# A decoder step on one core: operations listed first, issued at the end, with a table of moves on three engines

## The chip, the cores and the metric

One core of a Trainium2 chip runs the program. The time is the device time in microseconds (us) of one execution, the median of several. The engines are TensorE (PE in the profile, its weight loads PEld), VectorE (DVE), ScalarE (ACT), GpSimd (POOL) and SyncE (SP), whose queue issues all transfers. Each engine works through its own list of instructions in order; semaphores tie the lists together.

## The reference

One layer of a hybrid decoder, in float32, for 1024 tokens of a prompt and 8 single tokens of running sequences:

```python
p = x @ w_in                              # 1024 -> 9360 columns
p_gla, p_rwkv, p_gate = split(p)
o_gla  = gated linear attention of p_gla  # 4 heads, state 128 x 256, chunks
o_rwkv = RWKV-7 recurrence of p_rwkv      # 16 heads, state 64 x 64, token shift, group norm
m   = sigmoid(gate_a) * (o_gla @ w_up_gla) + sigmoid(gate_b) * (o_rwkv @ w_up_rwkv)
out = layernorm(alpha * x + m @ w_out)
```

The new states and the last shifted row are outputs too.

## The kernel before, in words

The prompt is worked in two passes of 512 tokens; the first also carries the 8 samples. Activations stand transposed: 128 columns of the projection on the partitions, tokens along the row. A float32 product is made of three products in a faster format: each operand is split into a high part (a cast on ACT: `xh`, `wpart`) and a low part (a subtraction on DVE: `xl`, `wpart`), and `hi*xh + hi*xl + lo*xh` is summed in a PSUM bank. `blocks` walks a plan of such 128-column blocks: first all of `w_in` for pass 0 and 1, then the two up-projections, then the output projection. A block takes a bank `proj` (2 of them) or `big` (5); `evacuate` copies the result out on ACT or DVE and frees the bank.

Beside this stream of large matmuls run, as Python generators, the small ones. `pair` handles two RWKV heads: `front` makes decays, keys (`kb`), the products `BK` (in tiles named `wide`) and `AZ` (`az`), and two sums over heads by a matmul with `headsr`, whose operand is split into two tiles `part`; the second of them sums `te`, a scalar_tensor_tensor of `r`, `rk` and `kb`. Four `big` banks of products are then masked into `gg`. `back` and `turn` invert small triangular blocks (`Xd`, `XT`, `Yd`) and turn the values; `chain` steps through 8 chunks with three matmuls each in the one bank `pch`; `norm` normalises and writes out. `gla_head` does the same for one attention head, `load_x` loads and splits the rows of the next stage's input.

What sets the order is the class `Order`. Every generator yields operations; each operation has an estimated cost and an estimated earliest start on its engine. `run` keeps asking all streams for their next operation, gives each a key (its start less a priority of its kind) and takes the smallest. So each engine's list is the order in which `run` took the operations. In the kernel before, `run` calls `op.fn()` at that moment, which issues the instruction. `take` hands out a buffer of a tag (the one idle longest by the estimates), `free` gives it back; the generators wait for buffers with `get`. All operations are issued through the same line of a helper, so nearly all instructions show one source line in the profile, and are told apart by their tiles.

Of the kernel before, what the change touches and what calls it, by code (L numbers as in the profile page):

```python
# [20 lines left out]
P = 128  # L21
# [73 lines left out]
STAND, SCARCE, PER_ROW = 0.033, 0.043, 0.107  # L95

URGENT = 1.952

STRETCH = 5
TUNED = {  # L100
# [29 lines left out]
SIGMOID, EXP = "sigmoid_and_others", "natural_log_exp_and_others"  # L130
# [45 lines left out]
class Op:  # L176


    def __init__(self, ways, out, ins, lag=0.0, table=None, tiles=None, port=""):
        self.ways, self.out, self.ins, self.lag, self.table, self.tiles = ways, out, ins, lag, table, tiles  # L180
        self.port, self.outs = port, [out]
        self.eng, self.fn, self.cost = ways[0]
# [123 lines left out]
class Order:  # L306
# [4 lines left out]
    def __init__(self, nc):  # L311
        self.P, self.A, self.V, self.G, self.S, self.E, self.C = (Engine(**e) for e in (
            {"P": nc.tensor}, {"A": nc.scalar}, {"V": nc.vector}, {"G": nc.gpsimd}, {"S": nc.sync},
            {"V": nc.vector, "G": nc.gpsimd}, {"A": nc.scalar, "V": nc.vector}))
        self.tiles = (P, P)
        self.quads = {"V": {}, "A": {}}
        self.time = dict.fromkeys("PAVGS", 0.0)
        self.port = dict.fromkeys("VG", 0.0)
        self.dma = 0.0
        self.flight = [0.0] * FLIGHT  # L320
        self.table = EXP
        self.ready, self.read = {}, {}
        self.streams, self.stretch = [], None
        self.tune(0)
        self.idle, self.make, self.home, self.wait = {}, {}, {}, {}
        self.kept, self.tile = {}, {}

    def tune(self, n):
# [4 lines left out]
            self.for_pe = {k: max(0.0, FOR_PE.get(k, 0.0) + x.get("pe " + k, 0.0)) for k in PRIO}  # L333

    def buffers(self, tag, bufs, make):
        self.idle[tag], self.make[tag], self.wait[tag] = [0.0] * bufs, make, 0

    def fixed(self, tag, tiles):

# [19 lines left out]
    def take(self, tag):  # L359
        idle = self.idle[tag]  # L360
        t = min(idle)
        idle.remove(t)
        x = self.make[tag]()
        self.home[x.tensor.name] = tag
        if tag in self.kept:
            self.tile[x.tensor.name] = x
        self.ready[x.tensor.name] = (t, None)
        return x

    def free(self, *xs):  # L370
        for x in xs:
            n = x.tensor.name
            tag = self.home.pop(n)
            self.idle[tag].append(max(self.ready.pop(n)[0], self.read.pop(n, 0.0)))
            if tag in self.kept:
                self.kept[tag].append(self.tile.pop(n))

# [21 lines left out]
    def start(self, op):  # L399

        best = None
        for eng, fn, cost in op.ways:
            free, t = self.time[eng] + (SWITCH if eng == "P" and op.tiles != self.tiles else 0.0), 0.0
            for x in (*op.outs, *op.ins):
                at, by = self.ready.get(x.tensor.name, (0.0, None))
                if eng == "S" and by == "D" and x is op.out:
                    continue
                if by != eng:
                    at += HOP.get(by, 0.0) + (SPARE if eng == "P" and by in ("V", "A", "G") else LANDED if by == "D" else 0.0)
                elif eng != "P" and x is not op.out:  # L410
                    at += AFTER[eng]
                t = max(t, at)
            t = max(t, *(self.read.get(x.tensor.name, 0.0) for x in (*op.outs, *(y for y in op.ins if y.space == PSUM))))
            if eng in op.port:
                free = max(free, self.port["G" if eng == "V" else "V"])
            if eng == "S":
                t = max(t, self.flight[-FLIGHT])
            late, t = free - t, max(t, free)
            if eng in "VA" and self.held(eng, op):
                cost += HOLD  # L420
            end = t + cost
            if len(op.ways) > 1:
                end += BIAS if eng == "V" and "A" in op.ways[0][0] else ASIDE if eng == "G" and "G" in op.port else 0.0
            if best is None or end < best[0]:
                best = end, t
                op.eng, op.fn, op.cost, op.late = eng, fn, cost, max(0.0, late)
        return best[1]
# [10 lines left out]
    def run(self):  # L438
        while self.streams:
            best, before = None, list(self.streams)  # L440
            self.urgent = self.needed()
            stand = max(STAND, SCARCE - PER_ROW * len(self.idle["row"]))
            for s in before:
                self.advance(s)
                if s.op is not None:
                    t = self.start(s.op)
                    if s.op.eng == "P":
                        key = t - stand * self.for_pe[s.kind] - (SWITCH if s.op.tiles != self.tiles else 0.0)
                    else:
                        key = t - self.prio[s.kind]  # L450
                    if s.kind in self.urgent:
                        key -= URGENT
                    if s.op.table not in (None, self.table):
                        key += max(0.0, TABLE - AGE * s.op.late)
                    if best is None or key < best[0]:
                        best = key, t, s
            if best is None:
                assert self.streams != before, "streams wait for one another"
                continue
            _, t, s = best  # L460
            op, s.op = s.op, None
            cost = op.cost
            if op.table not in (None, self.table):
                cost += TABLE
                self.table = op.table
                self.nc.scalar.preload_act_table_set(self.table)  # L466
            op.fn()
            self.time[op.eng] = max(self.time[op.eng], t + cost)
            if op.eng in op.port:
                self.port[op.eng] = t + cost  # L470
            if op.eng == "P":
                self.tiles = op.tiles
            elif op.eng in "VA":
                for x, q in self.starts(op):
                    self.quads[op.eng][x is op.out, x.space] = q
            end = t + cost
            if op.eng == "S":
                self.dma = max(self.dma, end) + op.lag[0]
                end = self.dma + op.lag[1]
                self.flight.append(end - EARLY)  # L480
            for x in op.outs:
                n = x.tensor.name
                self.ready[n] = max(end, self.ready.get(n, (0.0,))[0]), "D" if op.eng == "S" else op.eng
            for x in op.ins:
                n = x.tensor.name
                self.read[n] = max(self.read.get(n, 0.0), end)


class Kern(Order):
# [331 lines left out]
    def first_blocks(self, xs):  # L821

        run = []
        for b in self.plan[:2]:
            evac = yield from b.act()
            for tt, (t0, n) in enumerate(b.c.tiles):
                ps = yield from self.get("big")
                run.append((b, tt, t0, n, ps, evac))
        w, idle = {}, (yield from self.bank("pch", [P, P]))
        half = len(run) // 2  # L830
        for k, part in [(0, run[:half]), (1, run[:half]), (0, run[half:]), (1, run[half:])] + [(k, run) for k in range(2, NK)]:
            yield lambda: len(xs) > k
            for b, tt, t0, n, ps, evac in part:
                f0 = t0 - LEAD if b.lead and tt else t0
                q = ps[:, :t0 + n - f0]
                if tt == 0 and k % 4 == 0:
                    yield lambda: self.ws
                    w[id(b)] = self.ws.pop(0)
                hi, lo = (w[id(b)][:, v, k % 4 * P:k % 4 * P + P] for v in range(2))
                xh, xl = xs[k]  # L840
                yield self.P.matmul(q, hi, xh[:, f0:t0 + n], start=(k == 0), stop=False)
                yield self.P.matmul(q, hi, xl[:, f0:t0 + n], start=False, stop=False)
                yield self.P.matmul(q, lo, xh[:, f0:t0 + n], start=False, stop=(k == NK - 1))
                fin = tt == len(b.c.tiles) - 1
                if fin and k % 4 == 3:
                    yield from self.used(w[id(b)])
                if k == NK - 1:
                    self.spawn(self.evacuate(evac(tt, t0, n, q), ps, b.post if fin else None), "evacuate")
            for _ in range(IDLE if part is not run and part[0] is run[0] else 0):
                yield self.P.matmul(idle, self.warm, self.warm, start=True, stop=True)  # L850
            if k == 2:
                self.free(idle)
# [1104 lines left out]
```

## Time and profile before

| | us |
|---|---|
| median of 3 runs | 1434.02 (1433.89 to 1434.51) |
| the profiled execution, time | 1435.45 |
| the profiled execution, span | 1433.6 |
| PE busy in the span | 1417.2 |
| DVE, ACT, POOL busy | 1053.5, 827.3, 419.4 |
| granted TensorE clock, mean | 0.999 |

The span is from the first to the last instruction. "Busy" of PE is the time covered by at least one recorded matmul; since matmuls overlap in the record, a wait of PE shows there only with the part that no earlier matmul covers. A wait is named by the engine, the tile that the waiting instruction writes, and what ended the wait.

### The profile page before, as it was taken

Reading aid. Unit: us, or ns where it says so; the run is one execution under the profiler, and the core shown is the slowest. Engines: PE = TensorE matmul, PEld = TensorE weight load, DVE = VectorE, ACT = ScalarE, POOL = GpSimd, SP = SyncE. Lnnn points to the kernel's source line nnn. Section 1 sums busy time; section 2 is a strip of 40 time slices with the busy share of each in tenths; the row PEclk is TensorE's granted clock in tenths of the full one; section 3 lists DMA queues with packets and bytes.
Section 4 is the critical chain, followed back from the end, with each engine's and each line's share of the span. In section 5 each row is a group of like instructions: output and inputs, shape, how many; then the busy total and the mean of one; then the engine's idle time right before and its main releaser. Section 6 shows DMA issues by size and latency. Waiting matters only on the chain.

```text
span 1433.6 us, 30379 instructions
## 1 busy us (share of the span) xinstructions
PE 1417.2 (99%) x10640; PEld 1251.5 (87%) x10640; DVE 1053.5 (73%) x2125; ACT 827.3 (58%) x2070; POOL 419.4 (29%) x1156
## 2 busy tenths in 40 slices
PE   9999999999999999999999999999999999999997
PEld 8999999999999998888888887888888898897786
DVE  7688485978586978477668879788795946676685
ACT  6556666665658576556475646564667646654210
POOL 1060506261525250533512463265314050000000
PEclk9999999999999999999999999999999999999999
DMA  9798979686988786886688777577568597798732
GB/s 327 245 317 261 312 234 329 210 283 219 280 274 292 260 266 220 252 242 176 185 238 261 202 217 208 156 216 217 163 205 245 162 262 250 246 305 288 256 125 83
DMA packets 284789, 340.12 MB, mean 237 GB/s; under 512 B 159027, under 2 KB 174524, under 8 KB 284636
## 3 DMA queue, kind: packets, MB, share of 16 engines
q1 hardware_dynamic: 284636, 338.18, 75.0%
q8 instruction: 85, 1.39, 0.4%
q14 instruction: 68, 0.56, 0.1%
HBM read 210.03 MB, written 127.00 MB: 235 GB/s over the span
## 4 chain that ended last, share of the span: by engine, by line
PE 86%; DVE 6%; ACT 3%; DMA 2%; issue 1%; SPq 1%; POOL 0%; DVEq 0%; ACTq 0%; POOLq 0%
PE proj L273 54%; PE big L273 25%; PE pch L273 6%; DVE row L273 2%; ACT row L273 2%; DVE wide L273 1%; DVE wpart L273 1%; SPq L273 1%; DMA wraw<-w_in 1%; DVE gg L273 0%; DMA row<-lora 0%; ACT wpart L273 0%; ACT L466 0%; DVE Xd L273 0%; DVE XT L273 0%
## 5 line engine op out<-in xcount | busy, mean ns | idle before, releaser
L273 PE MATMUL proj<-xh,wpart 128*128 128x256 f32 (+3 forms) x3696 | 903.1, 329 | 0.9 <-DVE row L273 0.8
L273 PEld LDWEIGHTS proj<-xh,wpart 128*128 128x128 f32 x3696 | 617.2, 189 | 52.6 <-issue 5.5
L273 PE MATMUL proj<-xl,wpart 128*128 128x256 f32 (+3 forms) x1848 | 606.5, 328 | 0.1
L273 PEld LDWEIGHTS proj<-xl,wpart 128*128 128x128 f32 x1848 | 348.7, 189 | 26.9 <-issue 2.8
L273 POOL TENSOR_TENSOR Xt<-X,wide 128x60 f32<-128x60 f32 (+24 forms) x496 | 173.2, 349 | 285.3 <-DMA wide<-LD 201.5
L273 DVE TENSOR_TENSOR wpart<-wraw,wpart 128x512 fp32r<-128x512 f32 x206 | 143.6, 706 | 60.7 <-ACT wpart L273 52.9
L273 POOL TENSOR_TENSOR X<-X,Xt 128x60 f32<-128x60 f32 (+24 forms) x496 | 175.0, 353 | 38.7
L273 DVE TENSOR_TENSOR row<-row 128x256 f32<-128x256 f32 (+10 forms) x334 | 173.6, 533 | 11.5 <-ACT row L273 5.6
L273 ACT CAST wpart<-wraw 128x512 fp32r<-128x512 f32 x210 | 128.6, 620 | 73.9 <-PE proj L273 30.1
L273 ACT ACTIVATE row<-row 128x512 f32<-128x512 f32 (+5 forms) x229 | 138.0, 611 | 6.7 <-DVE row L273 3.9
L273 PE MATMUL big<-xh,wpart 128*128 128x256 f32 (+3 forms) x576 | 133.5, 319 | 0.2 <-DVE wpart L273 0.2
L273 POOL TENSOR_TENSOR row<-row 128x512 f32<-128x512 f32 (+4 forms) x35 | 40.0, 1153 | 300.7 <-DVE row L273 178.8
L273 ACT COPY row<-big 128x128 f32<-128x128 f32 (+6 forms) x187 | 61.9, 347 | 70.1 <-PE big L273 63.0
L273 PEld LDWEIGHTS big<-xh,wpart 128*128 128x128 f32 x576 | 95.3, 188 | 6.9 <-DVE wpart L273 0.4
L273 DVE TENSOR_TENSOR wide<-pch,gg 64x65 f32<-64x65 f32 x224 | 49.9, 223 | 60.1 <-PE pch L273 57.6
L273 PE MATMUL big<-xl,wpart 128*128 128x256 f32 (+3 forms) x288 | 91.7, 318 | 0.9 <-DVE xl L273 0.9
L273 DVE SCALAR_TENSOR_TENSOR row<-proj,pv,row 128x255 f32<-128x255 f32 (+1 forms) x95 | 54.6, 575 | 49.2 <-ACT tail L273 37.1
L273 ACT COPY rh<-pch 128x130 f32<-128x130 f32 x119 | 31.8, 267 | 96.3 <-PE pch L273 95.6
L273 ACT COPY wide<-pch 64x65 f32<-64x65 f32 x243 | 50.4, 207 | 51.4 <-PE pch L273 48.1
L273 PE MATMUL big<-row 128*64 128x64 f32 (+5 forms) x680 | 69.0, 287 | 0.1
L466 ACT ACT_TABLE_LOAD x52 | 66.7, 1283 | 0.9
L273 ACT ACTIVATE row<-proj,omu 128x256 f32<-128x256 f32 (+1 forms) x95 | 51.7, 544 | 23.3 <-PE proj L273 22.6
(222 smaller groups left out, 2044.3 us busy)
## 6 DMA issues: line engine op xcount, KB each, us to landing
w<-wpart SPq DMA_DIRECT2D x146, 512.0 KB
wpart<-w SPq DMA_DIRECT2D x146, 512.0 KB
wraw<-w_in SPq DMA_DIRECT2D x146, 256.0 KB
wide<-LD SPq DMA_DIRECT2D x64, 128.0 KB
BT<-row SPq DMA_DIRECT2D x32, 256.0 KB
wide<-BT SPq DMA_DIRECT2D x64, 128.0 KB
wraw<-w_up_gla SPq DMA_DIRECT2D x32, 256.0 KB
row<-w_out SPq DMA_DIRECT2D x32, 256.0 KB
```

Of the source, the lines that this page charges most:

```text
L273: ways.append((eng, lambda call=call: call(out, *args, **kw), price(eng, name, out, args, ins)))
L466: self.nc.scalar.preload_act_table_set(self.table)
```

## The change

`run` no longer issues. It appends each operation to a list, `issued`, with its engine, the names of the tensors that it writes and reads, and its table of functions on ACT. When all are listed, `issue` makes one list per engine, notes for every operation which earlier ones it needs (writers of what it reads or writes, readers of what it overwrites, and the last users of the buffer that its tile follows in, kept in `gone` and `follows`), and then edits the lists of PE ("P"), ACT ("A") and DVE ("V") by a table: an entry (n, k) takes the operation at place n and puts it back at place n + k. Then the lists are issued, always the earliest-listed operation that is next on its engine and whose needs are met. The operations, their engines, costs and the estimates by which `run` lists them are the same as before.

The table has 70 entries for PE, 50 for ACT and 109 for DVE; most places are 1 to 5. Two lines of it, and the new code:

```diff
+MOVES = {"P": [
+    (6, -4), (7, -4), (8, -4), (10, 4), (10, 3), (15, -4), (16, -4), (16, -1), (65, 3), (69, -3), (70, -2),
...
+         "V": [
...
+    (296, 2), (301, -1), (362, -2), (363, 4), (365, -1), (373, 2), (381, -4), (380, -2), (381, -2), (383, 2),
...
     def take(self, tag):
         idle = self.idle[tag]
         t = min(idle)
+        before = self.gone[tag].pop(idle.index(t))
         idle.remove(t)
         x = self.make[tag]()
+        self.follows[x.tensor.name] = before
...
             if op.table not in (None, self.table):
                 cost += TABLE
                 self.table = op.table
-                self.nc.scalar.preload_act_table_set(self.table)
-            op.fn()
+            self.issued.append((op.eng, op.fn, {x.tensor.name for x in op.outs}, {x.tensor.name for x in op.ins}, op.table))
...
+        self.issue()
+
+    def issue(self):
+
+        todo = {e: [] for e in "PAVGS"}
+        wrote, read, touch, needs = {}, {}, {}, []
+        for n, (eng, _, outs, ins, _) in enumerate(self.issued):
+            todo[eng].append(n)
+            need = {wrote[x] for x in outs | ins if x in wrote}
+            for x in outs | ins:
+                if x in self.follows and x not in touch:
+                    need.update(touch.get(self.follows[x], ()))
+                touch.setdefault(x, []).append(n)
+            for x in outs:
+                need.update(read.pop(x, ()))
+                wrote[x] = n
+            for x in ins - outs:
+                read.setdefault(x, []).append(n)
+            needs.append(need)
+        for eng, moves in MOVES.items():
+            for n, places in moves:
+                todo[eng].insert(n + places, todo[eng].pop(n))
+        loaded, done, at = EXP, set(), dict.fromkeys(todo, 0)
+        while len(done) < len(self.issued):
+            n = min(todo[e][k] for e, k in at.items() if k < len(todo[e]) and needs[todo[e][k]] <= done)
+            eng, fn, _, _, table = self.issued[n]
+            if table not in (None, loaded):
+                loaded = table
+                self.nc.scalar.preload_act_table_set(table)
+            fn()
+            done.add(n)
+            at[eng] += 1
```

Three places show what the table does to the lists. Buffer numbers differ between the two programs, so only the names and the order are to be compared.

The first is DVE in `front` of a pair in pass 0 (near 265 us in the trace of before). `pc` is a copy of decays, the four `wide` rows are the products into `BK`, the SCALAR_TENSOR_TENSOR is `te`, `part` the low part of its split, `Xd` the transposes of another pair's `back`. Before:

```order
L273 COPY pc_4079<-row_3829 128x8
L273 TENSOR_TENSOR wide_3813<-row_3830,row_3829 64x8x64
L273 TENSOR_TENSOR wide_3813<-row_3472,row_3829 64x8x64
L273 TENSOR_TENSOR wide_3813<-row_3830,row_3829 64x8x64
L273 TENSOR_TENSOR wide_3813<-row_3472,row_3829 64x8x64
L273 SCALAR_TENSOR_TENSOR row_3831<-row_3349,pv_88,row_3472 128x512
L273 TENSOR_TENSOR wpart_4069<-wraw_3976,wpart_4069 128x512
L273 TENSOR_TENSOR wpart_4132<-wraw_4010,wpart_4132 128x512
L273 TENSOR_TENSOR part_4124<-row_3831,part_4123 128x512
L273 STREAM_TRANSPOSE Xd0_184<-XT0_178 32x4x32 x4
```

and after:

```order
L303 COPY pc_812<-row_771 128x8
L303 TENSOR_TENSOR wide_763<-row_772,row_771 64x8x64
L303 TENSOR_TENSOR wide_763<-row_711,row_771 64x8x64
L303 SCALAR_TENSOR_TENSOR row_773<-row_693,pv_88,row_711 128x512
L303 TENSOR_TENSOR wide_763<-row_772,row_771 64x8x64
L303 TENSOR_TENSOR wide_763<-row_711,row_771 64x8x64
L303 TENSOR_TENSOR wpart_816<-wraw_803,wpart_816 128x512
L303 STREAM_TRANSPOSE Xd0_184<-XT0_178 32x4x32
L303 TENSOR_TENSOR part_815<-row_773,part_814 128x512
L303 STREAM_TRANSPOSE Xd0_184<-XT0_178 32x4x32
L303 TENSOR_TENSOR wpart_810<-wraw_797,wpart_810 128x512
```

`te` moved ahead of two of the products, and the second subtraction behind the `part` that follows from `te` and two transposes of `back`.

The second is DVE one pair later (near 340 us), where the four `big` banks are masked into `gg`; the TENSOR_TENSOR on `row` is the last product of `norm` for the pair before. Before:

```order
L273 STREAM_TRANSPOSE Xd0_184<-XT1_179 32x4x32 x4
L273 TENSOR_TENSOR row_4974<-row_4974,row_3698 128x512
L273 TENSOR_TENSOR gg_4970<-big_5283,cons_76 128x8x64
L273 TENSOR_TENSOR gg_4970<-big_5284,cons_76 128x8x64
L273 TENSOR_TENSOR gg_4970<-big_5285,cons_76 128x8x64
L273 TENSOR_TENSOR gg_4970<-big_5286,cons_76 128x8x64
L273 COPY S_5211<-big_5183 128x256
```

and after:

```order
L303 STREAM_TRANSPOSE Xd0_184<-XT1_179 32x4x32 x4
L303 TENSOR_TENSOR gg_941<-big_991,cons_76 128x8x64
L303 TENSOR_TENSOR gg_941<-big_992,cons_76 128x8x64
L303 TENSOR_TENSOR gg_941<-big_993,cons_76 128x8x64
L303 TENSOR_TENSOR gg_941<-big_994,cons_76 128x8x64
L303 COPY S_979<-big_975 128x256
L303 TENSOR_TENSOR row_944<-row_944,row_744 128x512
```

The product of `norm` moved behind the four maskings and a copy.

The third is PE in the up-projection of the RWKV part, pass 1 (near 1291 us): a block into a `big` bank, whose rows `x4` to `x7` are still being loaded and split, and the next block into `proj`. Before:

```order
L273 MATMUL big_17800<-xh4_17784,wpart_17683 128x512
L273 MATMUL big_17800<-xh5_17792,wpart_17683 128x512
L273 MATMUL big_17800<-xl5_17825,wpart_17683 128x512
L273 MATMUL big_17800<-xh5_17792,wpart_17683 128x512
L273 MATMUL big_17800<-xh6_17824,wpart_17683 128x512
L273 MATMUL big_17800<-xl6_17839,wpart_17683 128x512
```

and after:

```order
L303 MATMUL big_3054<-xh4_3050,wpart_3026 128x512
L303 MATMUL proj_3069<-xh0_3034,wpart_3029 128x512
L303 MATMUL proj_3069<-xl0_3035,wpart_3029 128x512
L303 MATMUL proj_3069<-xh0_3034,wpart_3029 128x512
L303 MATMUL proj_3069<-xh1_3037,wpart_3029 128x512
L303 MATMUL proj_3069<-xl1_3038,wpart_3029 128x512
L303 MATMUL big_3054<-xh5_3052,wpart_3026 128x512
L303 MATMUL proj_3069<-xh1_3037,wpart_3029 128x512
L303 MATMUL proj_3069<-xh2_3040,wpart_3029 128x512
L303 MATMUL proj_3069<-xl2_3049,wpart_3029 128x512
L303 MATMUL proj_3069<-xh2_3040,wpart_3029 128x512
L303 MATMUL big_3054<-xl5_3060,wpart_3026 128x512
```

Nine matmuls of the next block moved between `xh4` and `xl5`.

More of the change, by code (lines that the diff above doesn't have):

```diff
@@ L322, in __init__ @@
         self.ready, self.read = {}, {}
-        self.streams, self.stretch = [], None
+        self.streams, self.stretch, self.issued = [], None, []
         self.tune(0)
-        self.idle, self.make, self.home, self.wait = {}, {}, {}, {}
+        self.idle, self.make, self.home, self.wait, self.gone, self.follows = {}, {}, {}, {}, {}, {}
         self.kept, self.tile = {}, {}
@@ L335, in buffers @@
     def buffers(self, tag, bufs, make):
-        self.idle[tag], self.make[tag], self.wait[tag] = [0.0] * bufs, make, 0
+        self.idle[tag], self.make[tag], self.wait[tag], self.gone[tag] = [0.0] * bufs, make, 0, [None] * bufs
     def fixed(self, tag, tiles):
@@ L374, in free @@
             self.idle[tag].append(max(self.ready.pop(n)[0], self.read.pop(n, 0.0)))
+            self.gone[tag].append(n)
             if tag in self.kept:
```

25 rows, old and new, of the table MOVES are left out of this document.

## The prediction

> **What bounds the kernel now.** I read the page's totals first, then the busy time by stretches, then who TensorE (PE) waits for, and last the timeline at the longest of those waits.
>
> ```profile
> span 1433.6 us, 30379 instructions
> PE 1417.2 (99%) x10640; PEld 1251.5 (87%) x10640; DVE 1053.5 (73%) x2125; ACT 827.3 (58%) x2070; POOL 419.4 (29%) x1156
> PE 86%; DVE 6%; ACT 3%; DMA 2%; issue 1%; SPq 1%; POOL 0%; DVEq 0%; ACTq 0%; POOLq 0%
> ```
>
> PE is busy for 1417.2 of 1433.6 us, and 86% of the chain that ended last is PE's. So what an order of instructions can win is about the 16.4 us in which PE is idle; a shorter queue on any other engine counts only where PE waits for it.
>
> ```profile
> 260.00:280.00 20.00, 18.13 (x169) 16.74 (x168) 19.70 (x34) 12.15 (x28) 7.38 (x12) 1.00 0.65 215
> 880.00:910.00 30.00, 29.21 (x183) 22.22 (x182) 28.97 (x63) 20.10 (x48) 3.01 (x4) 1.00 0.63 190
> 1420.00:1433.60 13.60, 6.07 (x50) 5.82 (x48) 8.00 (x16) 0.50 (x2) 0.00 (x0) 0.91 0.16 59
> ```
>
> The columns are the stretch, its length, PE, PEld, DVE, ACT and POOL busy (instructions), granted clock, DMA share and GB/s. In the last 13.6 us PE has 7.5 us of idle time: the tail after the last matmul. No move of the table stands later than 1300 us, so these 7.5 of the 16.4 stay. From 260 to 280 us PE lacks 1.87 us while VectorE (DVE) works 19.70 of 20.00: there PE's feeder is full, and only the order of its work can help.
>
> ```profile
> PE big L273 <- ACT part L273: 2.8, 3, 1.1
> PE pch L590 <- DVE warm L587: 1.1, 1, 1.1
> PE big L273 <- DVE gg L273: 1.0, 1, 1.0
> PE big L273 <- DVE xl L273: 0.9, 2, 0.5
> PE proj L273 <- DVE row L273: 0.8, 1, 0.8
> PE big L273 <- DVE part L273: 0.5, 1, 0.5
> PE big L273 <- ACT row L273: 0.5, 1, 0.5
> PE big L273 <- DVE Xd L273: 0.4, 1, 0.4
> PE pch L273 <- DVE wide L273: 0.3, 1, 0.3
> PE big L273 <- DVE wpart L273: 0.2, 1, 0.2
> ```
>
> These are all the waits of PE that the profile lists: total us, count, longest. They sum to 8.5 us, of which 1.1 is the program's start. That leaves 7.4 us in 12 waits. Every one is for DVE or ACT, two of the three engines whose order changes; none is for a DMA.
>
> **The change, part by part.** It removes and adds no instruction: the numbers of matmuls, DVE, ACT, POOL and DMA instructions are the same, and POOL's and SP's queues keep their order. The listing itself costs nothing on the chip, since with an empty table each engine would get the same instructions in the same order. What is left is 169 places on PE, 294 on DVE and 124 on ACT that hold another operation than before.
>
> *Place 1, 266 us.* PE waits for a head sum of `front`: DVE makes `te` from `r`, `rk` and `kb` (the SCALAR_TENSOR_TENSOR row), ACT casts it to `part`, PE multiplies.
>
> ```profile
> 265.29 0.28 PE L273 MATMUL proj<-xl,wpart 128*128 128x256 f32 x1
> 266.62 0.50 PE L273 MATMUL big<-part,headsr 128*128 128x512 f32 x1 [1.05 <-ACT part L273]
> 261.45 3.70 DVE L273 TENSOR_TENSOR wide<-row 64x512 f32<-64x512 f32 x4
> 265.17 0.75 DVE L273 SCALAR_TENSOR_TENSOR row<-row,pv 128x512 f32<-128x512 f32 x1
> 265.95 0.62 ACT L273 CAST part<-row 128x512 fp32r<-128x512 f32 x1 [1.32 <-DVE row L273]
> L273 DVE TENSOR_TENSOR wide<-row 64x512 f32<-64x512 f32 x64 | 43.5, 715 | 0.3
> ```
>
> DVE works through four products into `wide` before `te`; two of them are now behind it. At their mean of 0.715 us `te` starts at least 1.4 us earlier, more than the 1.05 us that PE idled, and ACT was idle (1.32) just before, so the cast follows at once. The wait goes. What is late instead is `wide`, by one `te` (0.75 us); its reader is the group of small products four microseconds further on, and the two `wpart` subtractions that DVE does there were put apart by the same table. The same pair of moves (`te` ahead of two products) stands at the second of the three waits for `part`, at 403 us, so I take that one away as well.
>
> Matmuls are recorded longer than their distance, so the list shows less than PE lost: the two starts above are 1.33 us apart, where the list says 1.05. The rows of place 3 give the size: 0.39 us recorded where starts lie 0.23 apart. I add 0.16 us to each of the 12 waits, 1.9 us in all. The pool is then 7.4 + 1.9 = 9.3 us.
>
> *Place 2, 342 us.* PE waits for a `big` bank that DVE empties into `gg`.
>
> ```profile
> 340.76 0.28 PE L273 MATMUL proj<-xh,wpart 128*128 128x256 f32 x1
> 342.01 0.43 PE L273 MATMUL big<-Xd,Ld 128*32 128x128 f32 x8 [0.97 <-DVE gg L273]
> 339.62 1.73 DVE L273 TENSOR_TENSOR row<-row 128x512 f32<-128x512 f32 x1
> 341.28 2.47 DVE L273 TENSOR_TENSOR gg<-big,cons 128x512 f32<-128x512 f32 x4
> 339.53 1.28 POOL L273 TENSOR_TENSOR row<-row 128x512 f32<-128x512 f32 x1
> ```
>
> A product of `norm` that took 1.73 us stood before the four `gg` products (2.47 / 4 = 0.62 us each). It is now behind them, so the first `gg` can start at 339.62 and be done at 340.3, before PE asks at 340.9: 0.97 + 0.16 = 1.1 us gained. The 1.73 us is more than twice the 0.62 of the other product, and POOL's product began 0.09 us before it; if `gg`, standing there now, were held up in the same way it would end near 341.3, and the gain would be 0.1. I take 0.62, since its four rows are the nearest; the lower end stays for the range. The Trainium skill (SBUF — State Buffer, "Who interferes with whom") says that a VectorE instruction with two SBUF inputs excludes a GpSimd instruction that reads SBUF for its whole length, and one with a single SBUF input does not; `gg` has a PSUM and an SBUF input. The 1.73 us, a product of two SBUF rows, agrees with it; no row here shows a `gg` product beside POOL's. By that rule the gain here is the 1.1 us; with a lock for every product the sum below would be 1.0 us smaller.
>
> *Place 3, 1292 us.* PE waits for `xl5`, the low part of a loaded row.
>
> ```profile
> 1290.65 0.76 PE L273 MATMUL big<-xh,wpart 128*128 128x512 f32 x2
> 1291.94 0.50 PE L273 MATMUL big<-xl,wpart 128*128 128x512 f32 x1 [0.54 <-DVE xl L273]
> 1290.25 0.43 DVE L273 TENSOR_TENSOR row<-row 128x264 f32<-128x264 f32 x1
> 1290.60 0.69 DVE L273 TENSOR_TENSOR wpart<-wraw,wpart 128x512 fp32r<-128x512 f32 x1
> 1291.20 1.29 DVE L273 TENSOR_TENSOR xl<-row,xh 128x512 fp32r<-128x512 f32 x2
> ```
>
> Nine matmuls of the next block are put between `xh4` and `xl5`: 9 x 0.23 = 2.1 us of work that needs only rows 0 to 2 and the next weights, which DVE had ready at 1291.29 and now starts 0.35 us earlier, because the sum into `row` is put behind `xl7`. The whole wait, 0.54 + 0.16 = 0.7 us, is covered. On PE nobody is queued behind this but the same nine matmuls' old place. The other wait for `xl`, at 1239 us, is met by putting a product out of a `proj` bank behind `xl6` and `xl7`; such a product (0.715 us by the mean above) is longer than that wait (0.4). Both together 0.9 + 0.3 = 1.2 us.
>
> *The third wait for `part`, 544 us.*
>
> ```profile
> 540.70 2.41 DVE L273 TENSOR_TENSOR wpart<-wraw,wpart 128x512 fp32r<-128x512 f32 x2
> 543.03 0.74 DVE L273 SCALAR_TENSOR_TENSOR row<-row,pv 128x512 f32<-128x512 f32 x1
> 540.96 1.59 POOL L273 TENSOR_TENSOR row<-row 128x520 f32<-128x520 f32 x1 [17.02 <-ACT row L273]
> 544.47 0.50 PE L273 MATMUL big<-part,headsr 128*128 128x512 f32 x1 [0.92 <-ACT part L273]
> ```
>
> `te` now has one subtraction ahead of it, not two, and one of the `wide` products behind. Undisturbed it would end near 541.8, two microseconds earlier; but the second of the two subtractions took some 1.8 us (0.6 + 1.8 = 2.4) beside POOL's product, and `te` now stands in its place, so it may end near 543.1 instead of 543.8. Then 0.7 of 1.1 us are gained and 0.4 left. I take the 0.4.
>
> *The rest.* The waits for DVE `row` (277 us: the evacuation is put ahead of four operations), ACT `row` (221 us: a copy ahead of four) and `Xd` (474 us: `te` and two transposes ahead of a product) each have the late operation put ahead of one to four others; at 0.4 to 0.8 us they are no longer than one or two such operations, and I count them gone. At 894 and 907 us (`part` and `wide`, 0.8 + 0.3 = 1.1 us) DVE works 28.97 of 30 us and little stands before the late operation that was not there already; I count a third, so 0.75 stays. The wait for `wpart` in the first 6 us (0.36) I leave: dummy matmuls are put into it, and their own time (three there) is about as long.
>
> *The sum.* 9.3 - 0.4 - 0.75 - 0.36 = 7.8 us. Against it stand the operations put back. The dearest are two that free a PSUM bank.
>
> ```profile
> 460.77 0.69 ACT L273 ACTIVATE row<-big,b_gneps 128x512 f32<-128x512 f32 x1
> 465.11 0.61 ACT L273 CAST wpart<-wraw 128x512 fp32r<-128x512 f32 x1
> 670.92 0.69 ACT L273 ACTIVATE row<-big,b_gneps 128x512 f32<-128x512 f32 x1
> 674.70 0.58 ACT L273 ACTIVATE row<-proj 128x512 f32<-128x512 f32 x1
> ```
>
> The logarithm of `norm` reads its `big` bank at 460.77 and 670.92; it now stands right ahead of the second and fourth row, about 3.65 and 3.1 us later, and so long the bank stays taken. With four other `big` banks the cost lies between 0 and 6.8 us. I take 0.8, near the low end: of the 12 listed waits only two were ended by a bank coming free (277 and 342 us), though each bank is taken and freed many times, so most of such a delay is spare. 7.8 - 0.8 = 7.0 us. The profiled execution has a span of 1433.6 us and a time of 1435.45, its run being 1.4 above the median of the timed ones; the sum is made on the span (1426.6) and I carry the difference to the median: 1434.02 - 7.0 = **1427.0 us**.
>
> **The rivals.**
>
> *Given back.* What is won before 880 us (`part` 2.8, `gg` 1.0, `row` 0.8, ACT `row` 0.5, `Xd` 0.4, with 0.16 for each of the seven, less 0.4: 6.2 us) brings PE early to 880-910 us, where DVE has 1 us to spare in 30. If DVE doesn't come early too, PE waits there for what it won. For it: DVE's share. Against: DVE's backlog is itself made of PE's results (its own idle time in the span is 380 us), so it moves along. All of it given back leaves the 1.2 us of `xl`, 1432.8; three quarters given back 1431.2.
>
> *More.* All 9.3 us, and about 1 us of waits too short for the list: 1423.7. Against: the DVE row of 880-910 us.
>
> *It doesn't do what it says.* The order on the engines that PE waits for is set by what arrives, and each wait comes back beside the old place: within 1431.1 to 1436.9, my value 1434. For it: in 260-280 us DVE is full, and an operation put back there is only another's wait. Against: the three places, where the operation put back has no reader within a microsecond.
>
> *Slower.* The two bank releases above become PE waits at full price: +6.8 us, with nothing gained 1440.8. It decides from 7.8 + 2.9 = 10.7 us of new waits on, so it needs both and four more of their kind. Against: five banks, and two bank waits in the whole list.
>
> **How the numbers follow.** A measurement here can tell about 0.2%, 2.9 us. Forecast (1424.5 to 1430): 0.68. Given back: 0.13, of which 0.10 is still over 0.2%. No change: 0.10. More: 0.05. Slower: 0.04. So faster 0.83, same 0.13, slower 0.04. The range runs from 1423.5 (all gained) to 1431.5 (three quarters given back); the lower end of place 2 (1428.0) and the full bank price on half the gain lie inside.
>
> **What would show it.** In the changed kernel's waits of PE, ACT `part` falls from 2.8 us to under 0.6, DVE `gg`, `row`, `Xd` and ACT `row` are gone or under 0.2 each, `xl` is under 0.3; PE's busy time stays within 2 us of 1417.2, and the tail stays 7.5 us. From 880 to 910 us one wait of over 0.3 us stays. Wrong would be: a new wait of PE for a `big` bank near 465 or 674 us, or a sum of waits above 5 us with other names; a `gg` product of 1.7 us near 340; or PE's busy time rising as the waits fall.

## The result, and the profile after

The changed kernel took 1423.99 us (median of 5 runs, 1422.54 to 1424.16) against 1434.02 us before; the ratio of the runs is 0.9926, with a 95% interval of 0.9911 to 0.9940, which is 10.6 us or 1423.4. Forecast were 1427.0, most likely 1424.5 to 1430, at the widest 1423.5 to 1431.5. The sign was right and the gain half as large again as forecast. The median (1423.99) lies below the likely stretch, and the time by the ratio (1423.4) just below the widest one, where the rival "more" (1423.7) had been put.

The totals, and the stretches that answer to those of before (places now come up to 12 us earlier):

```profile
span 1421.0 us, 30372 instructions
PE 1411.5 (99%) x10640; PEld 1251.5 (88%) x10640; DVE 1050.7 (74%) x2125; ACT 829.7 (58%) x2070; POOL 419.6 (30%) x1156
...
PE 99%; DVE 0%; DMA 0%; ACT 0%; issue 0%; SPq 0%; DVEq 0%; ACTq 0%
```

```profile
260.00:280.00 20.00, 19.98 (x189) 19.04 (x187) 19.66 (x33) 12.46 (x31) 8.08 (x12) 1.00 0.66 219
870.00:900.00 30.00, 29.60 (x188) 23.17 (x187) 28.46 (x63) 21.05 (x51) 2.72 (x4) 1.00 0.66 192
1406.00:1421.00 15.00, 7.49 (x56) 6.93 (x54) 7.99 (x16) 0.50 (x2) 0.00 (x0) 0.90 0.20 72
```

The same instructions, 12.6 us less span. From 260 to 280 us PE now fills 19.98 of 20 us while DVE works 19.66, as much as before: only the order of its work differs. The tail (7.5 us without a matmul) is unchanged. The chain that ended last is now 99% PE.

All waits of PE in the changed kernel:

```profile
PE pch L654 <- DVE warm L651: 1.1, 1, 1.1
PE big L303 <- ACT xh L303: 0.5, 1, 0.5
PE big L303 <- DVE Xd L303: 0.4, 1, 0.4
```

Twelve waits behind the start became two: one for `xh` at 7 us, which the ninth run, the same kernel, does not have, and one at 878 us that is new. None is for a bank.

Where the time went is best read place by place: the start of PE's n-th matmul in one trace less that in the other grows in steps, and each step is one place. The middle column compares the traces of before and after. The right one compares a second pair: the program of before (the first run below) and the changed kernel once more (the ninth), whose profiled runs took 1433.8 and 1422.68 us, close to their medians.

| place, us | forecast | before, after | second pair |
|---|---|---|---|
| 6 to 40, start and `lora` | 0 | 0.6 | 0.3 |
| 76 and 124 | 0 | 0.6 | 0.6 |
| 199 | 0 | 0 | 0.8 |
| 221, ACT `row` | 0.7 | 0.7 | 0 |
| 266 `part` and 277 `row` | 2.2 | 2.3 | 2.3 |
| 342, `gg` | 1.1 | 1.0 | 0.2 |
| 403, `part` | 1.0 | 1.2 | 1.2 |
| 474, `Xd` | 0.6 | 0.5 | 0.5 |
| 544, `part` | 0.7 | 1.2 | 1.2 |
| 487, 609, 680 and 950 to 1180 (steps of up to 0.4) | 0 | 1.7 | 2.0 |
| 894 `part` and 907 `wide` | 0.4 | 1.0 | 0.6 |
| 1239 and 1292, `xl` | 1.2 | 1.6 | 1.6 |
| banks held longer | -0.8 | 0 | 0 |

The table leaves out steps under 0.1 us; the columns sum to 7.1, 12.4 and 11.3, where the whole distances are 7.0, 12.6 and 11.1. The profiled run of before was 1.4 us above its median, that of after 1.2 below: that is why the traces differ by more than the medians.

### The profile page after: what moved, and what is told of

Its sections match the earlier page's. It is cut to its first block, busy times and chain, and to the rows that moved or that the text cites. A ratio compares the mean times of both kernels' runs of the same rounds, so it can differ in the third digit from the quotient of the medians.

```text
span 1421.0 us, 30372 instructions
## 1 busy us (share of the span) xinstructions
PE 1411.5 (99%) x10640; PEld 1251.5 (88%) x10640; DVE 1050.7 (74%) x2125; ACT 829.7 (58%) x2070; POOL 419.6 (30%) x1156
## 4 chain that ended last, share of the span: by engine, by line
PE 99%; DVE 0%; DMA 0%; ACT 0%; issue 0%; SPq 0%; DVEq 0%; ACTq 0%
PE proj L303 65%; PE big L303 27%; PE pch L303 6%; DMA row<-xT 0%; DVE XT L303 0%; DVE row L303 0%; ACT row L303 0%; SPq L303 0%; DVE st L303 0%; ACT xh L303 0%; DVE Xd L303 0%; ACT l2p L303 0%; ACT tail L303 0%; DVEq L303 0%; ACTq L303 0%
## 5 line engine op out<-in xcount | busy, mean ns | idle before, releaser
L303 POOL TENSOR_TENSOR Xt<-X,wide 128x60 f32<-128x60 f32 (+24 forms) x496 | 170.3, 343 | 283.8 <-DMA wide<-LD 183.1
L303 POOL TENSOR_TENSOR X<-X,Xt 128x60 f32<-128x60 f32 (+24 forms) x496 | 178.2, 359 | 38.7
L303 PE MATMUL big<-xh,wpart 128*128 128x264 f32 (+3 forms) x576 | 133.5, 319 | 0.5 <-ACT xh L303 0.5
```

What stands on the lines that cost most here:

```text
L303: ways.append((eng, lambda call=call: call(out, *args, **kw), price(eng, name, out, args, ins)))
```

## The experiments

In every kernel here the computation is complete; only `MOVES` is edited. Gains at a place are steps as in the table, against the trace of before for the second to fourth run and against the first run for the others.

**1. Listing alone**

```diff
-MOVES = {"P": [...], "A": [...], "V": [...]}
+MOVES = {}
```

> The changed kernel with an empty table: operations are listed and issued at the end, nothing is moved. Theory (the moves alone make the gain): ratio 1.000 within 0.2%, the waits of PE those of before (12 after the start, 7.4 us), every matmul within 0.3 us of its start before. Rival (issuing late changes buffers or semaphores by itself): part of the 10 us shows here, a ratio under 0.998.

1434.48 us, ratio 0.9999 (0.9990 to 1.0007). The listing costs and wins nothing that can be measured; the gain is the moves. But the same program didn't wait at the same places. At 199 us it lost 0.86 that the trace of before hadn't lost, and at 342 us 0.24 where that lost 1.04. The two timelines, DVE and POOL, first of before:

```profile
197.62 0.69 DVE L273 TENSOR_TENSOR row<-row 128x512 f32<-128x512 f32 x1
196.25 1.31 POOL L273 TENSOR_TENSOR wpart<-wraw,wpart 128x512 fp32r<-128x512 f32 x1 [24.36 <-ACT wpart L273]
```

and of the same instructions in this run, with those at 340 us behind them:

```profile
197.29 1.60 DVE L275 TENSOR_TENSOR row<-row 128x512 f32<-128x512 f32 x1
197.06 1.29 POOL L275 TENSOR_TENSOR wpart<-wraw,wpart 128x512 fp32r<-128x512 f32 x1 [24.91 <-ACT wpart L275]
...
339.50 0.93 DVE L275 TENSOR_TENSOR row<-row 128x512 f32<-128x512 f32 x1
338.61 1.27 POOL L275 TENSOR_TENSOR wpart<-wraw,wpart 128x512 fp32r<-128x512 f32 x1 [21.23 <-ACT wpart L275]
339.84 1.74 POOL L275 TENSOR_TENSOR row<-row 128x512 f32<-128x512 f32 x1
```

Where POOL's product began first (by 0.23 us at 197, by 0.09 at 339 in the trace of before), DVE's took 1.6 to 1.7 us and POOL's 1.3; where they did not meet, DVE's took 0.69. At 339 us of this run DVE's began beside the last 0.38 us of one POOL product and 0.34 us before the next: it took 0.93, a little longer than alone, and the second POOL product 1.74. Which of the two is first differs from run to run, and at these two places PE's wait behind it does too. This agrees with the rule of the Trainium skill (SBUF — State Buffer, "Who interferes with whom") that the prediction weighed at 342 us.

**2 and 3. DVE's table alone; PE's and ACT's without DVE's**

```diff
-MOVES = {"P": [...], "A": [...], "V": [...]}
+MOVES = {"V": [...]}                 # the second run
+MOVES = {"P": [...], "A": [...]}     # the third
```

> Only the 109 moves of DVE's list; PE's and ACT's lists as before. In the traces of before and after, the start of the n-th matmul comes earlier by steps, 12.6 us in all. Theory (each place is a separate wait and the gains add): the steps at 266-277 (2.3), 342 (1.0), 403 (1.2), 474 (0.5), 544 (1.2), 602 and 681 (0.6), 894-907 (1.0), 1134 (0.3), 1239 (0.6), 76 and 124 (0.6) stay, those at 221 (0.7), 487 (0.3), 1087 (0.2) go, 34 (0.75) and 1292 (0.95) in part: 9 to 10.5 of 12.6 us in the profile, ratio 0.993 to 0.995. Rival (the three tables need each other, PE's order follows DVE's): under 6 us, ratio over 0.996.

1429.43 us, ratio 0.9966 (0.9954 to 0.9979).

> Only the 70 moves of PE's and the 50 of ACT's list; DVE's list as before. Theory (gains add): what the run with DVE's moves alone lacks, 2 to 3.5 us of 12.6, at 34 (part), 221 (0.7), 487 (0.3), 1087 (0.2), 1292 (up to 0.95); the waits for part, gg, Xd stay as before; ratio 0.9975 to 0.999. The bank price (the logarithm of norm 3.1 and 3.65 us later on ACT) would show here as new waits for a big bank near 465 and 674 us: none expected, since the changed kernel has none. Rival (tables need each other): no gain or a loss, ratio 1.000 or more.

1429.42 us, ratio 0.9965 (0.9951 to 0.9978). Each half is worth about 5 us, and both times lie outside what the theory expected: DVE's moves, to which it gave 9 to 10.5 of 12.6 us, make half. The second run is where the rival put it (over 0.996), but not for the rival's reason, since the other half alone gains as much. The sum of the two (0.0069) is the gain of the whole (0.0074) within the intervals, but place by place the halves don't add: either one alone wins the 0.5 us at 474, while 266 to 277 needs both for its 2.3. At 266 to 277 and at 403 us DVE's moves won 0.0 and -0.2 us, PE's and ACT's 1.4 and 1.2. The waits with DVE's moves alone:

```profile
PE big L287 <- DVE part L287: 1.8, 2, 1.1
PE proj L287 <- DVE row L287: 1.3, 1, 1.3
...
```

and the chain that ends at the first of them, on DVE, ACT and PE:

```profile
261.49 0.74 DVE L287 SCALAR_TENSOR_TENSOR row<-row,pv 128x512 f32<-128x512 f32 x1
262.26 2.29 DVE L287 TENSOR_TENSOR wide<-row 64x512 f32<-64x512 f32 x2
264.58 0.69 DVE L287 TENSOR_TENSOR wpart<-wraw,wpart 128x512 fp32r<-128x512 f32 x1
265.19 0.29 DVE L287 STREAM_TRANSPOSE Xd<-XT 32x128 f32<-32x128 f32 x1
265.42 0.64 DVE L287 TENSOR_TENSOR part<-row,part 128x512 fp32r<-128x512 f32 x1
...
259.69 1.28 ACT L531 ACT_TABLE_LOAD   x1
...
261.78 1.17 ACT L287 ACTIVATE row<-row 128x520 f32<-128x520 f32 x2
262.85 0.61 ACT L287 CAST wpart<-wraw 128x512 fp32r<-128x512 f32 x1
263.36 0.62 ACT L287 CAST part<-row 128x512 fp32r<-128x512 f32 x1
264.24 0.39 PE L287 MATMUL big<-part,headsr 128*128 128x512 f32 x1
...
266.11 0.50 PE L287 MATMUL big<-part,headsr 128*128 128x512 f32 x1 [0.65 <-DVE part L287]
```

`te` is done at 262.2 us, but ACT comes to its cast only at 263.36: ahead of it in ACT's list stand a table load and five operations. That delay costs PE nothing: it takes the high half at 264.24 without a wait. The low half, on DVE, could start when the cast ends (263.98), but stands behind two `wide` products, a subtraction and a transpose, starts at 265.42 and ends at 266.1. So PE waits for `DVE part` instead of `ACT part`. The wait changed its name.

At 342 us the second run and the changed kernel ("after", where the place has moved to 335 us) show `gg` beside POOL's product:

```profile
338.47 2.48 DVE L287 TENSOR_TENSOR gg<-big,cons 128x512 f32<-128x512 f32 x4
338.78 1.28 POOL L287 TENSOR_TENSOR row<-row 128x512 f32<-128x512 f32 x1
```

```profile
335.51 2.48 DVE L303 TENSOR_TENSOR gg<-big,cons 128x512 f32<-128x512 f32 x4
335.41 1.30 POOL L303 TENSOR_TENSOR row<-row 128x512 f32<-128x512 f32 x1
```

Four products in 2.48 us, 0.62 each as without a neighbour, and POOL's at its undisturbed 1.28 to 1.30. In the changed kernel POOL's began 0.10 us before `gg`, which is the case that the prediction feared. A product with one input in PSUM and one in SBUF did not wait, as the Trainium skill's rule above has it; the lower end of place 2 (a gain of 0.1 us because `gg` is held up) did not occur.

**4. The moves before 870 us only**

```diff
-MOVES = {"P": [...], "A": [...], "V": [...]}
+MOVES = {"P": [... to (5125, -2)], "A": [... to (1350, -1)], "V": [... to (1258, 2)]}
```

> All moves that stand before 870 us in the trace of before, none behind it. Theory (gains stay once they are won): 9.1 us in the profile at 870 us, 9.1 give or take 0.3 at the end, ratio 0.9935 to 0.995; the waits at 894 and 907 as before (0.67 and 0.46). Rival (given back at 880-910, where DVE works 28.97 of 30 us): the waits there grow to several us and at 920 us less than half of the 9.1 is left, ratio over 0.996.

1425.65 us, ratio 0.9940 (0.9928 to 0.9953). The trace is 9.0 us ahead at 692 us and 9.8 at the end, 0.7 more than expected; 0.5 of this is the wait at 894 us, which the first run didn't have either. The wait for `wide` near 897 us is 0.44 as before. What is won early is kept across the stretch where DVE is full. "Given back" falls.

**5, 6 and 7. Who decides the waits for `part`**

The place of `te` in DVE's list didn't. A new theory: ACT's list does. Eight of its moves put the chain of `front` that makes the inputs of its products (a logarithm, exponentials, the activation with `oka`) ahead of evacuations of `proj` banks.

```diff
-MOVES = {"P": [...], "A": [...], "V": [...]}
+MOVES = {"A": [...]}                                            # fifth: all 50 of ACT's
+MOVES = {"A": [(385, -2), (384, 2), (390, -2), (389, 2),        # sixth: eight of them
+               (612, -2), (613, -1), (617, -2), (617, -1)]}
+MOVES = {"P": [...], "A": [... without these eight], "V": [...]}  # seventh
```

> Only ACT's 50 moves. PE's and ACT's tables together gained 5.0 us, DVE's 4.9; with DVE's alone PE waited 0.8 us at 266 and 1.3 at 403 for the low part (DVE part) instead of the high one. New theory: the first two waits for part are decided on ACT, where the chain of front (square root, decays, the exponent times oka) is put ahead of evacuations, so that te starts over 1 us earlier. It expects both waits (1.2 and 1.0 us) gone here, those at 544 and 474 too or halved, 3 to 4 us in all, ratio 0.997 to 0.998. The prediction's theory (te's place on DVE decides): both waits as before, under 1.5 us, ratio over 0.9985.

1431.56 us, ratio 0.9981 (0.9972 to 0.9990). Won are 1.4 us at 266 and 1.2 at 403, as the new theory has it; the sum stays just under its 3 to 4 us, because operations put back cost about 0.5 us each at 392, 602 and 1136.

> Only eight of ACT's moves, at 255-259 and 393-396 us, those of the chain of front. New theory: the waits for part at 266 and 403 go, 2.2 to 2.6 us, ratio 0.998 to 0.9987, and nothing else changes by over 0.3 us. The prediction's theory: no change, ratio 1.000, both waits there.

1432.40 us, ratio 0.9985 (0.9976 to 0.9993). The waits of PE in the sixth run:

```profile
...
PE big L276 <- ACT part L276: 0.9, 1, 0.9
PE proj L276 <- DVE row L276: 0.8, 1, 0.8
...
PE big L276 <- DVE part L276: 0.5, 2, 0.3
...
PE proj L276 <- ACT row L276: 0.2, 1, 0.2
```

One wait for `ACT part` is left, that of 544 us; at 266 us 1.38 us are won and at 403 us 1.22, with eight moves of 229 and none of `te`. How they do it shows on DVE. In the trace of before DVE itself waited for ACT's rows on its way to `pc` and the `wide` products:

```profile
256.94 0.75 DVE L273 SCALAR_TENSOR_TENSOR row<-row,nkk 128x512 f32<-128x512 f32 x1 [0.60 <-ACT row L273]
...
258.96 0.69 DVE L273 SCALAR_TENSOR_TENSOR row<-row 128x512 f32<-128x512 f32 x1 [0.48 <-ACT row L273]
```

At 403 us the same two waits were 1.48 and 0.48 us. In the sixth run all four are gone, while a wait for `wpart` just ahead of them is 0.2 and 0.7 us longer. Counted from one of PE's matmuls (the one 40 places ahead of its first on `part`), `pc` starts 1.2 us earlier at 266 and 1.6 at 403 than in the first run, and the low half of `part`, which closes this row of DVE's operations, 1.4 and 1.5. In these figures 0.4 us is a delay of PE's own, told next; the tenth run, without that delay and with `te` in its old place, has 1.25 and 1.75 for `pc` and 1.6 at both for the low half.

The eight moves have a price of their own: the evacuations that were put back make PE wait 0.35 us at 256, and `DVE part` 0.36 at 392. Neither wait is in the changed kernel, where DVE's and PE's moves stand beside these.

> All moves but those eight of ACT's. New theory: PE waits again at 266 and 403, 0.8 and 1.3 us (as with DVE's moves alone), and at 277 for the row about 1.4, so 2 to 3.5 us of the 10.6 are lost: ratio 0.9940 to 0.9950. The prediction's theory: te is early enough by DVE's moves, under 0.5 us lost, ratio 0.9925 to 0.993.

1426.58 us, ratio 0.9945 (0.9932 to 0.9957), 2.7 us slower than the whole table. The waits:

```profile
PE proj L302 <- DVE row L302: 1.3, 1, 1.3
PE big L302 <- DVE part L302: 1.1, 1, 1.1
...
PE big L302 <- DMA row<-lora: 0.9, 1, 0.9
...
```

The `DVE part` at 402 us and the `row` at 278 are back, as with DVE's moves alone; at 266 us only 0.4 us is lost, where 0.8 was expected. The 0.9 us for the transfer of `lora` near 34 us is chance: by the distances of starts this place lost between 0 and 0.95 us in the runs, and nothing of the table was different there. So the eight moves are worth about 2.2 us alone and 2.7 among the others.

**8. Four places alone**

```diff
-MOVES = {"P": [...], "A": [...], "V": [...]}
+MOVES = {"P": [(7269, -9), ... (7277, -8)],
+         "V": [(501, 5), (1398, -2), (1399, 16), (1882, -5), (1884, -6), (1884, -5), (1887, 2)]}
```

> Moves of four places alone, each on the engine that the prediction named: the product of norm behind gg at 342, az and pc at 907, the sums, the weights and the product behind xl at 1239 (all DVE), and the nine matmuls of the next block on PE at 1292 (without the sum put behind xl7). Each is read in the profile by how much PE's n-th matmul comes earlier across the place. Prediction's theory: 342 1.0 to 1.1 where PE waited 1.0, whatever POOL does meanwhile (gg products of 0.62 us each); 907 0.3 to 0.6; 1239 0.5 to 0.65; 1292 0.4 to 0.95. Rivals: at 342 0.1, if gg is held up beside POOL's product as the product of norm was; at 1292 under 0.2, if the next weights come too late without DVE's move.

A single execution, 1432.67 us, read by its places and not by its time. Won at 342 us 0.23, which is all that PE waited there in the first run; at 907 0.28, at 1239 0.62, at 1292 0.93. No wait for `gg`, none for `wide`, and of the two for `xl` none at either place (the 0.3 that is left stands in the first 8 us). At these places the prediction had the engine and the operation right, without help from other entries, and at 1239 and 1292 us the size too; at 907 us the whole table wins 0.6, twice as much. The DVE move that the prediction thought useful at 1292 us is not needed.

**9, 10 and 11. The changed kernel again, without `te`, and with two moves more**

> The changed kernel once more, as the measure for the two runs beside it on the same chip: ratio 0.9926 within its interval (0.9911 to 0.994); in the profile the waits at 266, 277, 342, 403, 474, 544, 907, 1239 and 1292 us gone again, those by chance (a transfer of lora near 34 us, a product beside POOL's near 199 and 890 us) free to differ by up to 0.9 us each.

1423.05 us, ratio 0.9924 (0.9911 to 0.9936).

```diff
-    (362, -2), ... (584, -2),       # tenth: these two out of the whole "V"
+    (1363, 1), (384, -1)            # eleventh: behind the whole "V"
```

> All moves but the two that put te ahead of two products on DVE at 266 and 403 us. New theory (ACT's list decides these waits; its cast of part stands behind three others and starts over 2 us after te is done): nothing lost there, under 0.3 us at each place, ratio as the changed kernel's beside it. The prediction's theory: the waits for part come back, 2.4 us, ratio 0.0017 higher.

1423.01 us, ratio 0.9922 (0.9908 to 0.9935), the same as with them. The chain in that run, DVE and ACT:

```profile
262.76 1.69 DVE L303 SCALAR_TENSOR_TENSOR row<-row,pv 128x512 f32<-128x512 f32 x1
260.47 1.28 ACT L547 ACT_TABLE_LOAD   x1
...
262.67 1.17 ACT L303 ACTIVATE row<-row 128x520 f32<-128x520 f32 x2
263.88 0.62 ACT L303 CAST wpart<-wraw 128x512 fp32r<-128x512 f32 x1
264.49 0.62 ACT L303 CAST part<-row 128x512 fp32r<-128x512 f32 x1
```

`te` is now late, and even held up beside POOL (1.69 us), and still ends at 264.45, as ACT is done with what stands ahead of the cast (264.50). PE does not wait at either place. (Its profiled run lost 1.5 us at 152 us on a wait for `rh`, which is not in the other traces.)

> The changed kernel with two more moves on DVE, at waits that its profile still has: the last transpose of back ahead of a product of norm near 878 us (PE waits 0.47 for it) and the evacuation of a proj bank ahead of one more product near 275 us (0.18). Theory (local waits add): 0.65 us less, 0.0005 in the ratio, too little for the times; in the profile both waits gone and no other new. Rival (given back): a new wait of 0.3 us or more within 30 us behind one of the two places.

1422.21 us, ratio 0.9917 (0.9903 to 0.9930), the lowest of the three but inside the others' intervals. Its waits of PE beside the start:

```profile
PE pch L303 <- DVE wide L303: 0.2, 1, 0.2
```

The wait at 878 us (0.46 by the starts) is gone and nothing followed it, so that move is a gain that the trace shows and the times can't. The other was given back: 0.18 us less at 276 us, and 0.28 more for `wide` at 280, four us later. The rival was right there.

## Why the prediction was right or wrong

**What bounds the kernel: right.** PE was the bound; 7.4 us of listed waits, 7.5 of tail. The tail stayed to a tenth.

**The listing: right.** Ratio 0.9999.

**The pool, 9.3 us: nearly right for the listed waits.** The rows of the table that stand for listed waits sum to 9.5 us in the traces of before and after, where the sum counted on 7.8. In the second pair they sum to 7.6, because two of them (221 and 342) were waits that the trace of before had by chance. At 894 us, too, the first run lost 0.5 us less than that trace. The forecast took every wait of the one trace for a fixed one.

**Place 1: right sum, wrong cause.** The step that fails is "`te` starts at least 1.4 us earlier, more than the 1.05 us that PE idled, and ACT was idle (1.32) just before, so the cast follows at once. The wait goes." It follows the high half of the split and leaves out the low one, which DVE makes. With DVE's moves alone `te` did start earlier, counted from PE's matmuls as at the sixth run (2.5 us at 266, 1.4 at 403), and though the cast did not follow at once, the high half came in time. But `pc`, the four `wide` products, `te` and two more operations stand ahead of the low half in either order. Its start moved by 0.45 us at 266 and not at all at 403 (0.2 later), and PE waited 0.65 and 1.15 us for it. What brings the low half forward is that this whole row of DVE's operations starts earlier, and there DVE waited for ACT: eight of ACT's moves end those waits (1.1 us at 266, 2.0 at 403), with `te` in its old place. The second, sixth, seventh and tenth runs show it four ways: with DVE's moves PE waited for the other half of `part`; with eight of ACT's alone the waits went; without them the one at 403 us was back and 0.4 us at 266; without the moves of `te` nothing was lost. The prediction read DVE's moves at that place and not the entries of ACT's table eight us ahead of it. That the 2.2 us forecast for 266 and 277 came out at 2.3 is luck: other entries of the table won them.

**Place 2: right in cause, half right in size.** `gg` was not held up. But the 1.0 us of the trace was one outcome of the encounter with POOL; in the first run the same program lost 0.24.

**Place 3 and 1239 us: right**, 0.93 to 0.95 and 0.62 against 0.7 and 0.5.

**544, 894 and 907 us: too little.** Forecast were 0.7 and 0.4, won 1.2 and 0.6 to 1.0. At 544 us the prediction weighed only the place of `te` among its neighbours; in the changed kernel the operations from `pc` on start 2.9 us earlier, counted as above, and `te` ends 4.2 us earlier. "At 894 and 907 us ... little stands before the late operation that was not there already" overlooked that part of DVE's 28.97 us was again two products beside POOL's.

**The price of the banks, 0.8 us: wrong, it is nothing.** The logarithms come 4.2 and 3.5 us later, counted in PE's matmuls, so their banks are held that much longer, and no wait for a bank came up near 465 or 674 us, in any run. The third and fifth run, which have these moves without DVE's, show none either.

**Waits too short for the list, counted as nothing: the largest miss in the sum.** The step is "The pool is then 7.4 + 1.9 = 9.3 us": it corrects the 12 listed waits and puts every other wait of PE at nothing. Places at which PE waited 0.1 to 0.4 us gave 2.3 us in the traces (76, 124, and those between 487 and 1180) and 2.6 in the second pair, with 0.8 more at 199. The rival "more" had put about 1 us there. That its time (1423.7) was met is partly luck: it took all 9.3 us of the listed waits, where the second pair shows 7.6. From 7.0 to 11.1 in the second pair: +2.6 short waits, +0.8 at 199, +0.8 banks, +0.5 at 544, +0.2 at 894 to 907, +0.4 for `xl`, +0.3 at the start, less 0.7 and 0.9 at 221 and 342; the other places make the last 0.1.

**The rivals.** "Given back" fell in the fourth run (9.0 us at 692 us, 9.8 at the end) and was right at one place, 280 us in the eleventh. "Slower" and "no change" fell with the result.

**What would show it.** `part`, `gg`, `row` and ACT `row` are gone as forecast; a wait for `Xd` is there, but another one. It stands at 878 us, in the stretch that was 880 to 910 before, so one wait of over 0.3 us is left there as forecast, under another name. PE's busy time was to stay within 2 us of 1417.2 and fell to 1411.5: short waits lie inside it, since a matmul's record covers them.

**Open:** which of PE's 70 moves matter. Taken from the third and fifth run (0.9965 and 0.9981) they are worth 2 us with intervals as wide. Nine of them won 0.93 us at 1292 us in the eighth run; the others weren't run alone.

## What to carry to other kernels

An operation that ends a wait has two lists behind it, that of its own engine and that of the engine which feeds it; read what stands ahead of both, and do so for every operand that the waiting engine needs next. Moving one operation forward inside a full list does not bring forward what stands behind the whole group; look for the waits of that engine itself ahead of the group. Profile the same program twice before pricing its waits: a wait that only one trace has is not there to be won, and the start-to-start distance of the waiting engine's n-th instruction between two traces shows the short waits that a list of waits leaves out. When the order is a table, run parts of it: eight entries of 229 made about a quarter of the gain, and two that looked decisive made none that could be measured.

## What the runs showed of the hardware

The encounters of DVE and POOL were the largest part of the difference between the trace of before and the first run, which has the same order (0.8 us each at 199 and 342, 0.5 at 894): a DVE product of two SBUF rows took 0.69 us alone and 1.60 to 1.73 when POOL's began 0.09 to 0.23 us before it. Where it met only the last 0.38 us of a POOL product it took 0.93, and the POOL product that began 0.34 us after it took 1.74 instead of 1.28. A scalar_tensor_tensor of SBUF rows behaves like the product (0.75 alone, 1.69 beside POOL's). Each such encounter ahead of an operation that PE waits for moved PE by up to 0.9 us.

Four small matmuls whose operand comes by the transfer of `lora`, in the trace of before and of after:

```profile
33.51 1.58 PE L273 MATMUL big<-row 64*8 64x512 f32 x4
```

```profile
33.32 1.03 PE L303 MATMUL big<-row 64*8 64x512 f32 x4
```

After, they started in two pairs, 0.007 us apart within a pair and 0.43 from pair to pair; before, nearly one behind the other (0.43, 0.13 and 0.43). That one of the two transfers came late there is likely but not shown: the trace lists no wait at this place. If so, a late transfer of one row block costs the overlap of two matmuls as well as the wait.
